# A pipeline of one pair in the expert stage: gate and up products ahead of the previous pair's down products

## The chip, the cores and the metric

The kernel runs on one core of one Trainium2 chip. The metric is the device time of one execution in microseconds (us), the median over several runs. The engines are TensorE (PE in the rows; PEld are its weight loads), VectorE (DVE), ScalarE (ACT), GpSimd (POOL) and SyncE (SP), which issues most DMA transfers.

## The reference

The reference is two whole transformer blocks on 512 tokens of width 1024 (a mixer of two recurrences with two feed-forward parts, then a state-space and a sparse-attention branch, then a mixture of experts). Only the mixture of experts at the end of the second block is touched by the change. Each token has two of 32 experts:

```python
combine = jnp.sum(jax.nn.one_hot(ids, N_EXPERTS, dtype=jnp.float32) * wts[..., None], axis=1)
out = jnp.zeros((b * s, d), jnp.float32)
for e in range(N_EXPERTS):
    he = jax.nn.silu(t @ w_g[e]) * (t @ w_u[e])
    out = out + combine[:, e:e + 1] * (he @ w_d[e])
```

The matrices w_g and w_u are 1024 x 256 and w_d is 256 x 1024, in float32, so that one expert has 3 MiB of weights and all 32 have 96 MiB. They are read once in each execution. The result is scaled by a gate row (g2 in the kernel) and added to the residual.

## The kernel before

The program is written with a planner: every instruction names its tiles, the planner works out the dependences, and it lays down the order of each engine from its own estimate of durations (`schedule_with_timeline_sim=True`), taking what stands first in the program among what it holds to be ready. An instruction can so be drawn ahead of one that stands before it in the program.

The expert stage is `Moe.experts`. Experts are worked in pairs n = 0 to 15, two pairs make a quad q, and each expert has 64 places for tokens. A pair fills the 128 partitions: places of its first expert in the lower 64, of its second in the upper 64. The steps of a pair are these:

- `gather(q)`, once for a quad: VectorE makes one-hot rows `oh` of token against place (L2089), TensorE multiplies them with token numbers and weights (the index products, L2097), and POOL fetches the rows of the tokens from `n2d` in HBM into `xr` by an indirect DMA (L2103).
- `turn(n)`: eight transposes of `xr` on TensorE (L2119), copied to `xg` (L2120).
- Gate and up products (L2143): 16 matmuls with 64-column tiles, alternating between the two experts, whose halves of the array work side by side. Each shows as two records, so a pair has 32. They fill one PSUM bank `ph`: gate in the left half, up in the right.
- `h`: silu of the gate half on ScalarE (L2147), then a product with the up half and the combine weight on VectorE (L2155).
- Four transposes of `oh` to `ohT` (L2152), and two transposes of `h` (L2158), copied to `hT` by VectorE (L2160).
- Down products (L2168): 8 matmuls with 64-column tiles (16 records) in two halves f of 512 columns. VectorE scales each by `g2` (L2171), ScalarE rounds it to `yh` (L2172), and VectorE keeps the rest as `yl` (L2173).
- After the second pair of a quad, the scatter (L2182, L2183): 32 matmuls of 128-wide tiles that add `ohT` times `yh` and `yl` of both pairs into a PSUM bank for each of eight blocks, each added to `yac` by VectorE (L2184).

PSUM has four banks with the tag pa (`ph` and the down products), three with pb (index products, half of the turns, `ohT`, `h` transposes, scatter) and one with pf (the other half of the turns).

The weights come through a ring of nine 1 MiB buffers, `ew`. Part j of the weights is pair j // 6, expert j % 2 of the pair, and within the pair two parts of gate and up (each two transfers of 512 KB, L2067) and then one of down (one transfer of 1024 KB, L2070). A tenth load takes the slot of the first when that has been used, and so on. `prefetch` asks for the first nine parts before the stage; `experts` asks for the parts of a pair at its head:

```python
for j in range(e0 * 3, e0 * 3 + 6):
    self.load(i, ew, j)
wts = [self.ewt.pop(j) for j in range(e0 * 3, e0 * 3 + 6)]
```

Between `gather(0)` and the first turn stands `then()`, a branch for experts with more than 64 tokens, whose body isn't entered here. Ahead of the stage, `tail2` stores the normed tokens to `n2d` with four transfers (L2304), from which POOL gathers.

Of the kernel before, what the change touches and what calls it, by code (L numbers as in the profile page):

```python
# [10 lines left out]
F32 = mybir.dt.float32  # L11
F32R = mybir.dt.float32r
# [3 lines left out]
AF = mybir.ActivationFunctionType  # L16
# [1943 lines left out]
class Moe:  # L1960
# [94 lines left out]
    def load(self, i, ew, j):  # L2055


        nc = self.nc
        if j >= NE * 3 or j in self.ewt:
            return  # L2060
        e, part = j // 6 * 2 + j % 2, j % 6 // 2
        t = ew.tile([128, 2048], F32, name="ew", bufs=EW)
        if part < 2:

            t = t.rearrange("p (n k m) -> p n k m", n=2, k=4)
            for n, w in enumerate(("w_exp_gate_2", "w_exp_up_2")):
                nc.sync.dma_start(t[:, n], i[w][0][e].rearrange("(p k) n -> p k n", k=8)[:, part * 4:part * 4 + 4])  # L2067
        else:
            t = t.rearrange("p (k n) -> p k n", k=2)
            nc.sync.dma_start(t, i["w_exp_down_2"][0][e].rearrange("(k p) n -> p k n", p=128))  # L2070
        self.ewt[j] = t

    def prefetch(self, i, ew):
        for j in range(EW):
            self.load(i, ew, j)

    def experts(self, i, ew, n2d, yac, xr, g2, then):

        nc, tc = self.nc, self.tc
        with tc.tile_pool(name="eb", bufs=1, reuse_waits="tile") as eb:  # L2080
            batch = []
            ohs, w2s, rows = {}, {}, {}

            def gather(q):

                oh = eb.tile([128, 4, 256], F32R, name="oh", bufs=2)
                ohs[q] = oh
                for c in range(4):
                    nc.vector.tensor_tensor(  # L2089
                        oh[:, c, :].rearrange("p (e s) -> p e s", s=CAP),  # L2090
                        self.pos[:, c, q * 4:q * 4 + 4][:, :, None].to_broadcast([128, 4, CAP]),
                        self.iota[:, None, :].to_broadcast([128, 4, CAP]), op=OP.is_equal)
                for pr in range(2):
                    n = q * 2 + pr
                    pw = self.pt("pb")
                    for c in range(4):
                        nc.tensor.matmul(pw[:, :6], oh[:, c, pr * 128:pr * 128 + 128],  # L2097
                                         self.chl[:, c, n].rearrange("p a b -> p (a b)"), start=(c == 0), stop=(c == 3))

                    ix = eb.tile([128, 16], U32, name="ix", bufs=4)[:, :1]  # L2100
                    nc.vector.tensor_scalar(ix, pw[:, 4:5], 512.0, None, op0=OP.add)
                    rows[n] = xr[:, n % 4, :]
                    nc.gpsimd.indirect_dma_start(rows[n], None, n2d, bass.IndirectOffsetOnAxis(ap=ix, axis=0),  # L2103
                                                 bounds_check=L - 1, oob_is_err=False)
                    w2 = w2s[n] = eb.tile([128, 16], F32, name="w2", bufs=4)[:, :1]
                    w4 = eb.tile([128, 16], F32, name="w4", bufs=2)[:, :4]
                    nc.vector.tensor_copy(w4, pw[:, :4])
                    for x in range(2):
                        rs = slice(x * 64, x * 64 + 64)
                        nc.vector.tensor_add(w2[rs, :], w4[rs, x:x + 1], w4[rs, 2 + x:3 + x])  # L2110

            def turn(n):

                r = rows.pop(n)
                for f in range(2):
                    p = self.pt(("pf", "pb")[f])
                    for k in range(4):
                        k4 = f * 4 + k
                        nc.tensor.transpose(p[:, k * 128:(k + 1) * 128], r[:, k4 * 128:(k4 + 1) * 128], self.ident)  # L2119
                    (nc.vector.tensor_copy if f else nc.scalar.copy)(  # L2120
                        xg4[:, n % 4, f * 4:f * 4 + 4, :], p.rearrange("p (k s) -> p k s", k=4))
            gather(0)
            then()
            self.table("silu_and_others")
            yhl = self.mo.tile([128, 2, 2, D], F32R, name="yhl", tag="H", bufs=1)
            xg4 = self.mo.tile([128, 4, 8, 128], F32, name="xg", tag="P", bufs=1)
            turn(0)
            for q in range(8):
                if q < 7:
                    gather(q + 1)  # L2130
                oh = ohs.pop(q)
                for pr in range(2):
                    e0 = q * 4 + pr * 2
                    for j in range(e0 * 3, e0 * 3 + 6):
                        self.load(i, ew, j)
                    wts = [self.ewt.pop(j) for j in range(e0 * 3, e0 * 3 + 6)]
                    ss = slice(pr * 128, pr * 128 + 128)
                    xg, w2 = xg4[:, (q * 2 + pr) % 4], w2s.pop(q * 2 + pr)

                    ph = self.pt("pa")  # L2140
                    for k in range(8):
                        for x in range(2):
                            nc.tensor.matmul(ph[x * 64:x * 64 + 64, :], xg[:, k, x * 64:x * 64 + 64],  # L2143
                                             wts[k // 4 * 2 + x][:, :, k % 4, :], start=(k == 0), stop=(k == 7),
                                             tile_position=(0, x * 64))
                    h = eb.tile([128, 256], F32, name="h", bufs=2)
                    nc.scalar.activation(h, ph[:, :256], AF.Silu)  # L2147
                    if e0 < 30:
                        turn(e0 // 2 + 1)
                    pt_ = self.pt("pb")  # L2150
                    for c in range(4):
                        nc.tensor.transpose(pt_[:, c * 128:(c + 1) * 128], oh[:, c, ss].bitcast(F32), self.ident)  # L2152
                    ohT = eb.tile([128, L], F32R, name="ohT", bufs=4)
                    nc.scalar.copy(ohT, pt_)
                    nc.vector.scalar_tensor_tensor(h, h, w2, ph[:, 256:], op0=OP.mult, op1=OP.mult)  # L2155
                    p = self.pt("pb")
                    for k in range(2):
                        nc.tensor.transpose(p[:, k * 128:(k + 1) * 128], h[:, k * 128:(k + 1) * 128], self.ident)  # L2158
                    hT = eb.tile([128, 2, 128], F32, name="hT", bufs=2)
                    nc.vector.tensor_copy(hT, p[:, :256].rearrange("p (k s) -> p k s", k=2))  # L2160
                    yh, yl = yhl[:, pr, 0, :], yhl[:, pr, 1, :]
                    for f in range(2):
                        fs = slice(f * 512, f * 512 + 512)
                        p = self.pt("pa")
                        for k in range(2):
                            for x in range(2):
                                dn = wts[4 + x]
                                nc.tensor.matmul(p[x * 64:x * 64 + 64, :], hT[:, k, x * 64:x * 64 + 64], dn[:, k, fs],  # L2168
                                                 start=(k == 0), stop=(k == 1), tile_position=(0, x * 64))
                        t = eb.tile([128, 512], F32, name="yt", bufs=2)  # L2170
                        nc.vector.tensor_mul(t, p, g2[:, fs])  # L2171
                        nc.scalar.copy(yh[:, fs], t)  # L2172
                        nc.vector.tensor_sub(yl[:, fs], t, yh[:, fs].bitcast(F32))  # L2173
                    batch.append((ohT, yh, yl))

                for c in range(4):
                    for f in range(2):
                        fs = slice(f * 512, f * 512 + 512)
                        p = self.pt("pb")
                        for n, (ohT, yh, yl) in enumerate(batch):  # L2180
                            s = slice(c * 128, (c + 1) * 128)
                            nc.tensor.matmul(p, ohT[:, s], yh[:, fs], start=(n == 0), stop=False)  # L2182
                            nc.tensor.matmul(p, ohT[:, s], yl[:, fs], start=False, stop=(n == len(batch) - 1))  # L2183
                        nc.vector.tensor_add(yac[:, c, fs], yac[:, c, fs], p)  # L2184
                batch = []

    def overflow(self, i, nT, yac, g2):

# [74 lines left out]
class Tail:  # L2263
# [21 lines left out]
    def tail2(self, i, mo, out):  # L2285
# [4 lines left out]
        yac = self.slot("yac", "B", True, F32)  # L2290
        xr = self.slot("xr", "A", True, F32)
        nc.gpsimd.memset(xr, 0.0)
        self.ewt = {}
        with tc.tile_pool(name="ea", bufs=1, reuse_waits="tile") as ea:
            self.room(mo)
            logits = self.logits(i, mo, self.nT, rt)
# [285 lines left out]
```

## Time and profile before

| what | us |
| --- | --- |
| median of 3 runs | 2822.51 |
| lowest and highest run | 2817.71 and 2826.92 |
| the profiled execution's own time | 2825.73 |
| its span | 2822.3 |
| first and last gate and up product | 2518.5 and 2793.1 |
| last scatter product starts | 2807.2 |

The span is the time from the first to the last profiled instruction; the execution's own time also holds what lies around it. TensorE is busy for 94% of the span by its records, whose ends are modelled. In the rows, a line such as L2168 is a line of the kernel before, `x16` counts records, and a text such as `[0.43 <-DVE hT L2160]` says that the engine had been idle for 0.43 us, and what ended that.

### The profile page before, as it was taken

To read this page: it belongs to the slowest core of one execution; us is meant where nothing else is said; L and a number is where in the kernel's file an instruction comes from. 1 tells how busy PE (TensorE), PEld (TensorE's weight loads), DVE (VectorE), ACT (ScalarE), POOL (GpSimd) and SP (SyncE) were. 2 spreads that over 40 slices of the span, in tenths; PEclk is the share of its full clock that TensorE was granted. 3 is DMA by queue.
4 is the path that set the end of the run, shared out by engine and by line. 5 is a ranking of instruction groups with operands and counts; after the bars stand their busy time and mean duration, and the time that the engine had idled before them with its cause. 6 is when DMAs were issued, how large, how long until landed. Compare 5 with 4: busy or idle time off the path is not lost. (4 is left out here: it accounts for less than half of the span.)

```text
span 2822.3 us, 40820 instructions
## 1 busy us (share of the span) xinstructions
PE 2664.6 (94%) x16161; PEld 2056.1 (73%) x16162; DVE 1552.3 (55%) x3022; ACT 993.5 (35%) x1786; POOL 284.6 (10%) x320
## 2 busy tenths in 40 slices
PE   7999999999998887999999899999999989979997
PEld 5788888888887765678888678777777767854443
DVE  6333333338367895554435757676667764454444
ACT  5211112225235663422223424465444443231112
POOL 2000000002001220100000101121122230010000
PEclk8999999999989998999999999999999999989999
DMA  7422222134333227832333523301234358269995
GB/s 263 150 90 68 59 61 67 46 98 119 96 100 106 65 66 259 278 97 90 100 95 90 150 83 99 91 13 36 79 101 124 97 187 255 81 244 360 363 371 196
DMA packets 340995, 380.46 MB, mean 135 GB/s; under 512 B 21817, under 2 KB 252605, under 8 KB 340546
## 3 DMA queue, kind: packets, MB, share of 16 engines
q1 hardware_dynamic: 338498, 373.63, 41.0%
q0 software_dynamic: 2304, 4.20, 0.4%
q8 instruction: 128, 2.10, 0.3%
q14 instruction: 65, 0.53, 0.1%
HBM read 352.34 MB, written 29.63 MB: 135 GB/s over the span
## 5 line engine op out<-in xcount | busy, mean ns | idle before, releaser
L193 ACT CAST whi<-wraw 128x1024 fp32r<-128x1024 f32 x277 | 285.7, 1041 | 739.6 <-PE pppa L213 327.2
L212 PE MATMUL pppa<-lath,whi 128*128 128x512 f32 (+4 forms) x1344 | 520.6, 388 | 18.8 <-ACT whi L193 5.3
L213 PE MATMUL pppa<-latl,whi 128*128 128x512 f32 (+3 forms) x1344 | 517.2, 385 | 5.9 <-DVE latl L360 3.8
L214 PE MATMUL pppa<-lath,wlo 128*128 128x512 f32 (+3 forms) x1344 | 510.6, 382 | 0.0
L194 DVE TENSOR_TENSOR wlo<-wraw,whi 128x1024 fp32r<-128x1024 f32 (+1 forms) x273 | 332.9, 1226 | 245.7 <-ACT whi L193 241.9
L212 PEld LDWEIGHTS pppa<-lath,whi 128*128 128x128 f32 (+3 forms) x1344 | 254.4, 189 | 81.4 <-ACT whi L193 11.6
L213 PEld LDWEIGHTS pppa<-latl,whi 128*128 128x128 f32 (+2 forms) x1344 | 254.1, 189 | 61.1 <-DVE latl L360 6.2
L214 PEld LDWEIGHTS pppa<-lath,wlo 128*128 128x128 f32 (+2 forms) x1344 | 253.5, 189 | 51.1 <-issue 2.7
L213 PE MATMUL pppb<-hl,whi 128*128 128x512 f32 (+1 forms) x576 | 195.7, 342 | 0.0
L212 PE MATMUL pppb<-hh,whi 128*128 128x512 f32 (+1 forms) x576 | 193.2, 345 | 0.0
L214 PE MATMUL pppb<-hh,wlo 128*128 128x512 f32 (+1 forms) x576 | 190.8, 340 | 0.0
L418 DVE SCALAR_TENSOR_TENSOR xT<-pppb,sG,xT 128x512 f32<-128x512 f32 (+1 forms) x144 | 96.7, 689 | 137.2 <-PE pppb L214 137.0
L398 DVE TENSOR_TENSOR hf<-sg,pppa 128x256 f32<-128x256 f32 (+1 forms) x68 | 39.7, 584 | 228.5 <-PE pppa L214 227.2
L212 PE MATMUL pppf<-lath,whi 128*128 128x512 f32 x320 | 128.1, 400 | 7.1 <-ACT lath L1835 3.4
L212 PE MATMUL pppa<-ctxh,whi 128*128 128x256 f32 (+1 forms) x440 | 124.8, 284 | 8.5 <-DVE W L921 8.2
L212 PEld LDWEIGHTS pppb<-hh,whi 128*128 128x128 f32 x576 | 108.3, 189 | 28.3 <-issue 5.8
L2143 PE MATMUL pppa<-ew,xg 128*64 128x512 f32 x512 | 127.3, 603 | 0.0
L214 PE MATMUL pppf<-lath,wlo 128*128 128x512 f32 x320 | 126.6, 396 | 0.6 <-DVE wlo L194 0.6
L213 PE MATMUL pppf<-latl,whi 128*128 128x512 f32 x320 | 126.7, 396 | 0.1
L213 PE MATMUL pppa<-ctxl,whi 128*128 128x256 f32 (+1 forms) x440 | 124.5, 283 | 0.3 <-POOL ctxl L358 0.3
L214 PE MATMUL pppa<-ctxh,wlo 128*128 128x256 f32 (+1 forms) x440 | 124.6, 283 | 0.0
L213 PEld LDWEIGHTS pppb<-hl,whi 128*128 128x128 f32 x576 | 108.9, 189 | 15.4 <-issue 3.4
(696 smaller groups left out, 4998.0 us busy)
## 6 DMA issues: line engine op xcount, KB each, us to landing
wraw<-in_ffn_w_dram SPq DMA_DIRECT2D x132, 512.0 KB, 4.1
wraw<-in_w_in_dram SPq DMA_DIRECT2D x102, 512.0 KB, 4.0
ew<-in_w_exp_gate_dram SPq DMA_DIRECT2D x64, 512.0 KB, 8.4
ew<-in_w_exp_up_dram SPq DMA_DIRECT2D x64, 512.0 KB, 4.7
ew<-in_w_exp_down_dram SPq DMA_DIRECT2D x32, 1024.0 KB, 11.0
mraw<-in_w_mod_dram SPq DMA_DIRECT2D x40, 512.0 KB, 6.0
wraw<-in_w_mod_dram SPq DMA_DIRECT2D x32, 512.0 KB, 4.5
mraw<-in_w_ada_dram SPq DMA_DIRECT2D x32, 512.0 KB, 5.7
```

Of the source, the lines that this page charges most:

```text
L193: nc.scalar.copy(hi[:, :n], raw[:, :n])
L194: (nc.gpsimd if pool else nc.vector).tensor_sub(lo[:, :n], raw[:, :n], hi[:, :n].bitcast(F32))
L212: nc.tensor.matmul(out, wh, xh, start=start, stop=False)
L213: nc.tensor.matmul(out, wh, xl, start=False, stop=False)
L214: nc.tensor.matmul(out, wl, xh, start=False, stop=stop)
L398: nc.vector.tensor_mul(h[:, :n], sg[:, :n], pp[1])
L418: nc.vector.scalar_tensor_tensor(x[:, o, :], p[:, :n], gate[:, o:o + 1], x[:, o, :], op0=OP.mult, op1=OP.add)
L2143: nc.tensor.matmul(ph[x * 64:x * 64 + 64, :], xg[:, k, x * 64:x * 64 + 64], wts[k // 4 * 2 + x][:, :, k % 4, :], start=(k == 0), stop=(k = ...
```

## The change

The loop over quads and pairs becomes a loop over 17 steps n. Step n runs `hidden(n)` (gate and up products, silu, turn of pair n + 1, the transposes of `oh` and `h`, the copy to `hT`) and then `output(n - 1)` (down products, scaling, rounding, and after an odd pair the scatter). `gather` stands ahead of `hidden` of an even pair, as before. The instructions themselves are the same.

The loads are asked for in the new order of use: the gate and up parts of pairs 0 and 1 (eight parts) in `prefetch`, and behind `hidden(n)` the down parts of pair n and the gate and up parts of pair n + 2. A set `ewd` keeps a part from being loaded twice. The ring still has nine buffers.

```diff
     def prefetch(self, i, ew):
-        for j in range(EW):
+        for j in range(4):
+            self.load(i, ew, j)
+        for j in list(range(6, 10)):
             self.load(i, ew, j)
...
+            def hidden(n):
+                for j in range(n * 6, n * 6 + 4):
+                    self.load(i, ew, j)
+                w = [self.ewt.pop(j) for j in range(n * 6, n * 6 + 4)]
...
+                h = eb.tile([128, 256], F32, name="h", bufs=2)
+                nc.scalar.activation(h, ph[:, :256], AF.Silu)
+                if n < 15:
+                    turn(n + 1)
...
+                hT = eb.tile([128, 2, 128], F32, name="hT", bufs=2)
+                nc.vector.tensor_copy(hT, p[:, :256].rearrange("p (k s) -> p k s", k=2))
+                hid[n] = hT, ohT
+
+            def output(n):
+                for j in range(n * 6 + 4, n * 6 + 6):
+                    self.load(i, ew, j)
+                w = [self.ewt.pop(j) for j in range(n * 6 + 4, n * 6 + 6)]
+                hT, ohT = hid.pop(n)
...
+                batch.append((ohT, yh, yl))
+                if n % 2 == 0:
+                    return
...
+                batch.clear()
+            for n in range(17):
+                if n < 16:
+                    if n % 2 == 0 and n < 14:
+                        gather(n // 2 + 1)
+                    hidden(n)
+
+                    for j in [n * 6 + 4, n * 6 + 5] + list(range(n * 6 + 12, n * 6 + 16)):
+                        self.load(i, ew, j)
+                if n:
+                    output(n - 1)
```

## Rows read from the trace of the kernel before

**Rows 1.** The page: its first line.

```profile
span 2822.3 us, 40820 instructions
```

**Rows 2.** Windows of two pairs: length, busy time (records) of each engine, clock, DMA.

```profile
core 0: us, PE busy (x) PEld busy (x) DVE busy (x) ACT busy (x) POOL busy (x), PEclk, DMA share, GB/s
...
2643.23:2680.56 37.33, 36.26 (x166) 16.46 (x164) 15.96 (x35) 5.58 (x10) 1.98 (x2) 1.00 0.93 351
2680.56:2716.35 35.79, 34.72 (x166) 16.37 (x164) 15.87 (x35) 5.58 (x10) 1.98 (x2) 1.00 0.97 366
...
sum 216.26, PE 210.75 PEld 98.00 DVE 93.31 ACT 34.08 POOL 9.90; mean PE 35.13 PEld 16.33 DVE 15.55 ACT 5.68 POOL 1.65
```

**Rows 3.** Timeline of TensorE, pairs 7 and 8: start, length, instruction, records, idle before.

```profile
2651.56 0.38 PE L2158 MATMUL pppb<-ident,h 128*128 128x128 f32 x2
2651.78 0.60 PE L2119 MATMUL pppf<-ident,xr 128*128 128x128 f32 x4
2652.14 0.48 PE L2182 MATMUL pppb<-yhl,ohT 128*128 128x512 f32 x1
...
2653.74 3.65 PE L2168 MATMUL pppa<-ew,hT 128*64 128x512 f32 x16 [0.43 <-DVE hT L2160]
2657.33 0.50 PE L2182 MATMUL pppb<-yhl,ohT 128*128 128x512 f32 x1
...
2657.99 4.50 PE L2143 MATMUL pppa<-ew,xg 128*64 128x512 f32 x18
...
2664.76 1.07 PE L2143 MATMUL pppa<-ew,xg 128*64 128x512 f32 x2
2665.76 0.51 PE L2182 MATMUL pppb<-yhl,ohT 128*128 128x512 f32 x1
...
2676.06 0.38 PE L2158 MATMUL pppb<-ident,h 128*128 128x128 f32 x2
2677.08 3.65 PE L2168 MATMUL pppa<-ew,hT 128*64 128x512 f32 x16 [0.64 <-DVE hT L2160]
2680.56 7.04 PE L2143 MATMUL pppa<-ew,xg 128*64 128x512 f32 x32
```

**Rows 4.** Waits, 2515 to 2800 us: who waited for whom, us, times, longest.

```profile
PEld pppa L2168 <- DVE hT L2160: 10.3, 13, 0.9
...
PE pppa L2168 <- DVE hT L2160: 6.0, 11, 0.6
...
PEld pppa L2143 <- DMA ew<-in_w_exp_down_dram: 2.5, 7, 0.4
...
PE pppb L2158 <- DVE h L2155: 2.0, 2, 1.0
```

**Rows 5.** Timeline of TensorE in pairs 13 and 15.

```profile
2761.05 0.48 PE L2182 MATMUL pppb<-yhl,ohT 128*128 128x512 f32 x1
...
2762.16 3.65 PE L2168 MATMUL pppa<-ew,hT 128*64 128x512 f32 x16
...
2794.73 0.44 PE L2158 MATMUL pppb<-ident,h 128*128 128x128 f32 x2 [1.00 <-DVE h L2155]
```

**Rows 6.** DMA queues, 2523.65 to 2786.69 us.

```profile
DMA packets 26320, 94.58 MB, mean 360 GB/s; under 512 B 3268, under 2 KB 3268, under 8 KB 26304
```

**Rows 7.** Windows, one of 20 us inside the stage.

```profile
2690.00:2710.00 20.00, 19.57 (x80) 8.69 (x79) 8.81 (x16) 1.96 (x4) 0.00 (x0) 1.00 1.03 409
```

**Rows 8.** The line L2067, gate and up weights: from issue to landing.

```profile
DMA to landing us min/median/max: 4.7/8.4/11.6
```

**Rows 9.** Timeline of SP's DMA issues.

```profile
2498.30 1.58 SPq L2304 DMA_DIRECT2D n2d<-n  x2
...
2657.42 0.33 SPq L2067 DMA_DIRECT2D ew<-in_w_exp_gate_dram  x1
```

**Rows 10.** Timelines of POOL and TensorE at the start of the stage.

```profile
2510.52 1.22 POOL L2103 DMA_INDIRECT xr<-n2d,ix  x1 [27.92 <-SPq L2194]
...
2515.15 1.09 PE L2119 MATMUL pppf<-ident,xr 128*128 128x128 f32 x4 [8.51 <-DMA xr<-n2d,ix]
```

More of the change, by code (lines that the diff above doesn't have):

```diff
@@ L2058, in load @@
         nc = self.nc
-        if j >= NE * 3 or j in self.ewt:
+        if j >= NE * 3 or j in self.ewt or j in self.ewd:
             return
+        self.ewd.add(j)
         e, part = j // 6 * 2 + j % 2, j % 6 // 2
@@ L2127, in experts @@
             turn(0)
[L2128 to L2141, printed above, removed]
-                        for x in range(2):
[L2143 to L2174, printed above, removed]
@@ new lines, in experts @@
+            hid, wts = {}, {}
+            def hidden(n):
+                for j in range(n * 6, n * 6 + 4):
+                    self.load(i, ew, j)
+                w = [self.ewt.pop(j) for j in range(n * 6, n * 6 + 4)]
+                xg, w2, oh = xg4[:, n % 4], w2s.pop(n), ohs[n // 2]
+                ph = self.pt("pa")
+                for k in range(8):
+                    for x in range(2):
+                        nc.tensor.matmul(ph[x * 64:x * 64 + 64, :], xg[:, k, x * 64:x * 64 + 64],
+                                         w[k // 4 * 2 + x][:, :, k % 4, :], start=(k == 0), stop=(k == 7),
+                                         tile_position=(0, x * 64))
+                h = eb.tile([128, 256], F32, name="h", bufs=2)
+                nc.scalar.activation(h, ph[:, :256], AF.Silu)
+                if n < 15:
+                    turn(n + 1)
+                pt_ = self.pt("pb")
+                for c in range(4):
+                    nc.tensor.transpose(pt_[:, c * 128:(c + 1) * 128],
+                                        oh[:, c, n % 2 * 128:n % 2 * 128 + 128].bitcast(F32), self.ident)
+                ohT = eb.tile([128, L], F32R, name="ohT", bufs=4)
+                nc.scalar.copy(ohT, pt_)
+                nc.vector.scalar_tensor_tensor(h, h, w2, ph[:, 256:], op0=OP.mult, op1=OP.mult)
+                p = self.pt("pb")
+                for k in range(2):
+                    nc.tensor.transpose(p[:, k * 128:(k + 1) * 128], h[:, k * 128:(k + 1) * 128], self.ident)
+                hT = eb.tile([128, 2, 128], F32, name="hT", bufs=2)
+                nc.vector.tensor_copy(hT, p[:, :256].rearrange("p (k s) -> p k s", k=2))
+                hid[n] = hT, ohT
@@ new lines, in output @@
+            def output(n):
[3 more added lines that the diff above has]
+                hT, ohT = hid.pop(n)
+                yh, yl = yhl[:, n % 2, 0, :], yhl[:, n % 2, 1, :]
+                for f in range(2):
+                    fs = slice(f * 512, f * 512 + 512)
+                    p = self.pt("pa")
+                    for k in range(2):
+                        for x in range(2):
+                            nc.tensor.matmul(p[x * 64:x * 64 + 64, :], hT[:, k, x * 64:x * 64 + 64], w[x][:, k, fs],
+                                             start=(k == 0), stop=(k == 1), tile_position=(0, x * 64))
+                    t = eb.tile([128, 512], F32, name="yt", bufs=2)
+                    nc.vector.tensor_mul(t, p, g2[:, fs])
+                    nc.scalar.copy(yh[:, fs], t)
+                    nc.vector.tensor_sub(yl[:, fs], t, yh[:, fs].bitcast(F32))
+                batch.append((ohT, yh, yl))
+                if n % 2 == 0:
+                    return
@@ L2179, in experts @@
                         p = self.pt("pb")
-                        for n, (ohT, yh, yl) in enumerate(batch):
+                        for m, (ohT, yh, yl) in enumerate(batch):
                             s = slice(c * 128, (c + 1) * 128)
-                            nc.tensor.matmul(p, ohT[:, s], yh[:, fs], start=(n == 0), stop=False)
-                            nc.tensor.matmul(p, ohT[:, s], yl[:, fs], start=False, stop=(n == len(batch) - 1))
+                            nc.tensor.matmul(p, ohT[:, s], yh[:, fs], start=(m == 0), stop=False)
+                            nc.tensor.matmul(p, ohT[:, s], yl[:, fs], start=False, stop=(m == len(batch) - 1))
                         nc.vector.tensor_add(yac[:, c, fs], yac[:, c, fs], p)
-                batch = []
+                batch.clear()
[8 more added lines that the diff above has]
+                    output(n - 1)
     def overflow(self, i, nT, yac, g2):
@@ L2292, in tail2 @@
         nc.gpsimd.memset(xr, 0.0)
-        self.ewt = {}
+        self.ewt, self.ewd = {}, set()
         with tc.tile_pool(name="ea", bufs=1, reuse_waits="tile") as ea:
```

## The prediction

> **What bounds the kernel now.** I read the page first: the span is 2822.3 us [rows 1], and its last ninth (2515 to 2807 us) is the expert stage, the only code that the diff touches. The windows come next, cut where the gate and up products of every second pair begin, so that one window is two pairs [rows 2]. The reader is to see a steady machine: six windows take 216.26 us, 36.04 us each, and TensorE is busy for 210.75 us of them at a granted clock of 1.00, the higher level (2.4 GHz). VectorE and ScalarE are busy for less than half of that, so neither is the bound. The DMA share is above 0.9, so the weights need a look of their own. The table of waits [rows 4] settles that TensorE does not wait for weights: the largest wait put down to a weight transfer is 2.5 us in all, of at most 0.4 us, which is the pause that stands at every change of product kind anyway. The transfers could go faster, too: a 20 us stretch moved 409 GB/s [rows 7] where the stage's mean is 360 GB/s [rows 6]. So TensorE's own stream bounds the stage, and I read it instruction by instruction [rows 3], taking the distance from one start to the next, since the ends are modelled.
>
> Three kinds of lost time are in that stream. First, the down products (L2168) wait for hT, the VectorE copy of the transposes just ahead of them. In an even pair the two h transposes start at 2676.06 and the down products at 2677.08 [rows 3]: 1.02 us, where two transposes take 0.22 us (2651.56 to 2651.78). In an odd pair a stopgap of four scatter products stands between, and still 1.60 us pass from 2652.14 to 2653.74, where the same four take 1.11 us in pair 13, which has no wait [rows 5]. Second, changes of kind. Down products followed by scatter take 3.59 us to the next start (2653.74 to 2657.33), followed by gate products 3.48 us (2677.08 to 2680.56), so going to 128-wide tiles costs 0.11 us; two scatter products take 0.46 us and 0.66 us pass before the gate products behind them (2657.33 to 2657.99), so coming back costs 0.20 us. Third, scatter products cut into the gate products of the next pair: two records at 2664.76 hold TensorE until 2665.76, 1.00 us, where two of an uncut row take 0.43 us (3.48 us over 16). The two 64-column halves, one per expert, run side by side, and the cut leaves one alone.
>
> **The change part by part.** All sums are made against the profiled execution: its span is 2822.3 us, its own time 2825.73 us, 3.2 us above the median of 2822.51 us. I take the same difference off the median.
>
> Removed: the wait for hT. In the new order the down products of pair n-1 follow the h transposes of pair n, and their hT was copied a whole set of gate products earlier. Even pairs (2, 4, ... 12): 1.02 - 0.22 = 0.80 us, less the 0.2 us that a change of kind costs anyway, is 0.6 us, six times: 3.6 us. Odd pairs with the wait (3, 5, 7, 9, 11): 1.60 - 1.11 = 0.5 us, five times: 2.5 us. Pair 14 has about half of one, 0.3 us. Together 6.4 us. The table of waits bounds it: 6.0 us on the matmul rows and 10.3 us on the weight loads [rows 4], which hold the pause of the change of kind as well, so I stay near the lower one. What is late next: nothing on VectorE waits for the moved work, and the hT copy gets some 8 us of slack.
>
> Removed too: in pairs 1 and 15 TensorE waits for h itself, 2.0 us in both [rows 4], 1.00 us in pair 15 [rows 5]. Pair 1 now has the down products of pair 0 beside it, and pair 15 those of pair 14. The h transposes can then cut into these, so I take 1.5 us of the 2.0.
>
> Added: the gather's index products (L2097) for the quads 2 to 7 stood behind the long run of scatter products, among 128-wide work. In the new order the down products of an even pair and the gate products of the next one are their neighbours, both 64 wide. That is one more change there and back, 0.11 + 0.20 = 0.3 us, six times: 1.8 us.
>
> Moved at no cost: the scatter stays behind the down products of the odd pair and ahead of the same gate products, so its cuts stay, with bounds: all of them gone saves at most about 2.3 us a window (the 1.54 us by which the fourth window is shorter than the third [rows 2], the same work with fewer cuts, and the rest in changes of kind), over seven scatters 16 us; as many again cost the same 1.5 us in each of eight, 12 us. I take 0, because both ends of each scatter have the neighbours they had.
>
> Weights: the order of fetching becomes the order of use again, and a ring of nine still hands each slot on nine loads later, so a load gets the same head start. One gate load issued at 2657.42 [rows 9] is for pair 9, whose products start at 2680.56 [rows 3], 23 us later, and the slowest such transfer landed 11.6 us after its issue [rows 8]. A window shorter by 1 us takes 1 us from a slack of about 11. SP issues the same 160 transfers; its waits are for slots, and behind it no compute engine waits. Cost 0; were the cover gone, a window would last as long as its 12.58 MB, 30.8 us at 409 GB/s, still below 35 us.
>
> Start of the stage: TensorE begins at 2515.15 when a gather by POOL, started at 2510.52 [rows 10], has landed; that waits for the token rows n2d, whose last two stores were issued at 2498.30 [rows 9], behind nine buffers of weights. The new prefetch loads eight. If the ninth falls behind the stores, 1 MB less stands ahead of them, 2.6 us at 409 GB/s. Nothing holds the ninth back, its slot being free, so I take 0 and keep 2.6 us as the gain's bound.
>
> Sum: -6.4 - 1.5 + 1.8 = -6.1 us. That makes 2819.6 us of the profiled 2825.7, and from the median 2816.4: **2816 us**. A window goes from 36.0 to about 35.2 us.
>
> A rule to weigh. The Trainium skill (DMA: Bandwidth & Descriptors, Bandwidth) says that for loads from HBM a limit of about 358 GB/s per core binds. By it the 94.58 MB of this stretch need 264 us, an estimate from that page, and the stretch has 263: nothing could be gained. The trace does not bear the rule out, with 409 GB/s for 20 us [rows 7]; by that row the same bytes need 231 us, and the sum stands.
>
> **The rivals.**
> 1. The scatter cuts fall away or grow fewer. The order on TensorE is a planner's, made from its own durations; in new company it may give the scatter an uncut run. For it: windows of the same work already differ by 1.5 us [rows 2]. Against: the cause of the cuts, waiting for the second pair's yh and yl, is unchanged. Two thirds of 16 us gone: 2816 - 10 = 2806 us.
> 2. The start comes earlier by the 2.6 us above: 2813.5 us.
> 3. Slower: the h transposes cut into the down products. Behind gate products now stand transposes, h transposes, down products of n-1. Where the planner holds h for late, it starts the down products, which are always ready, and lets h break in. Place: between the halves of one product pair. Price of one break: two halves alone, 0.85 us more (1.00 less about 0.15 for the change is a full slot for half a pair, twice), and a change there and back, 0.3 us: 1.15 us. In 16 pairs 18 us: 2816 + 18 = 2834 us. It eats the gain from 5 breaks on and makes the kernel measurably slower from 13. For it: pairs 1 and 15 show h late by 1 us where no transposes stand between [rows 5]. Against: in the odd pairs h follows twelve transposes with no pause (2651.56 [rows 3] bears no wait).
> 4. The weights bind: if the mean of 360 GB/s were a ceiling, the stretch could not shrink: 2822.5 us. The rule above says so in other words. For it: the DMA share of 0.9 and more [rows 2]. Against: rows 7 and the head start of 23 us.
> 5. The change does not do what it says: the planner already draws work ahead, and could draw pair n's down products back to where they were: 2822.5 us. Against: it takes what stands first in the program and is ready, and the down products of n-1 always are.
>
> **How the numbers follow.** Chances: the forecast 0.50 (own range 2811 to 2820, the hT term between 6.0 and 10.3 us and cuts a little either way), rival 1 0.15, rival 2 0.09, rival 3 0.14, rival 4 0.06, rival 5 0.06. About 0.3% (8.5 us) is what a measurement of this kernel can tell from no change: 2814.0 to 2831.0. Faster: 0.15 of the forecast's 0.50, all of rival 1 and most of rival 2, 0.37. Slower: most of rival 3, 0.12. Within: 0.51. The range 2805 to 2828 leaves out the far half of rival 1 and rival 3 with ten breaks and more.
>
> **What would show it.** Right: no wait of the down products for hT in the table of waits; a start of down products 0.2 to 0.3 us behind the h transposes; two-pair windows near 35.2 us; index products between down and gate products. Cuts right: as many short groups of gate products as before. Start: gather issue still near 2510.5. Wrong: groups of down products of fewer than 16 records with h transposes between them (rival 3); windows under 34 us (rival 1); waits of gate products for weights above 0.5 us (rival 4).

## The result, and the profile after

The changed kernel takes 2837.58 us (median of 8 executions, 2833.31 to 2839.84), the kernel before 2821.94 us (8 executions too, 2817.71 to 2826.92): a ratio of 1.0052 (95%: 1.0042 to 1.0062), so 15.6 us slower. The forecast was 2816 us and no measurable change. It went the way of rival 3, at 2834 us.

The page of the changed kernel begins so; span and share of TensorE answer to [rows 1] and to the table of the profile before:

```profile
span 2835.8 us, 40822 instructions
## 1 busy us (share of the span) xinstructions
PE 2678.7 (94%) x16161; PEld 2055.8 (72%) x16162; DVE 1551.1 (55%) x3022; ACT 992.8 (35%) x1786; POOL 281.9 (10%) x320
```

TensorE shows 94% as before, so the page alone hides the loss. The windows of two pairs, from the gate products of pair 2 to those of pair 14, answer to [rows 2]:

```profile
core 0: us, PE busy (x) PEld busy (x) DVE busy (x) ACT busy (x) POOL busy (x), PEclk, DMA share, GB/s
2539.81:2576.66 36.85, 36.85 (x162) 16.05 (x158) 13.60 (x29) 5.58 (x10) 1.98 (x2) 1.00 1.03 409
...
2617.15:2659.69 42.54, 42.34 (x185) 19.38 (x185) 18.41 (x48) 6.19 (x13) 3.95 (x4) 1.00 0.86 315
...
sum 229.44, PE 227.37 PEld 103.93 DVE 95.22 ACT 33.65 POOL 11.86; mean PE 37.90 PEld 17.32 DVE 15.87 ACT 5.61 POOL 1.98
```

The six take 229.44 us, 38.2 us each where 35.2 was forecast. Those of [rows 2] took 216.26, but begin one pair later; from pair 2 to pair 14 the kernel before took 218.5 us (2547.88 to 2766.40). The clock is 1.00 as before. TensorE counts as busy for all but 2 us of them: before it idled 5.5 us and was faster. The time is inside the busy records, so the timeline has to show it (down products of pair 7, gate products of pairs 8 and 9; it answers to [rows 3]; the first column is the start):

```profile
2659.69 7.09 PE L2142 MATMUL pppa<-ew,xg 128*64 128x512 f32 x32
2666.61 1.88 PE L2175 MATMUL pppa<-ew,hT 128*64 128x512 f32 x4
2668.42 0.44 PE L2158 MATMUL pppb<-ident,h 128*128 128x128 f32 x2
2668.61 0.48 PE L2190 MATMUL pppb<-yhl,ohT 128*128 128x512 f32 x1
...
2670.18 3.65 PE L2175 MATMUL pppa<-ew,hT 128*64 128x512 f32 x12
2673.76 0.74 PE L2190 MATMUL pppb<-yhl,ohT 128*128 128x512 f32 x2
2674.43 1.07 PE L2142 MATMUL pppa<-ew,xg 128*64 128x512 f32 x2
2675.43 0.73 PE L2191 MATMUL pppb<-yhl,ohT 128*128 128x512 f32 x2
...
2685.62 0.66 PE L2122 MATMUL pppb<-ident,xr 128*128 128x128 f32 x4
2686.11 0.60 PE L2151 MATMUL pppb<-ident,oh 128*128 128x128 f32 x4
2686.64 3.65 PE L2142 MATMUL pppa<-ew,xg 128*64 128x512 f32 x16
```

L2175 is the down products, L2158 the h transposes, L2142 the gate and up products, L2190 and L2191 the scatter, L2122 the turn, L2151 the transposes of `oh`. The 16 records of a pair's down products (a product leaves two) took 3.48 us to the next start before. Here four take 1.81 us (2666.61 to 2668.42) and twelve 3.58 (2670.18 to 2673.76), 5.39 us together, because the h transposes stand between. Side by side, four records would take 0.85 us and twelve 2.6. The order of the program's TensorE instructions says why. H stands for the h transposes, S6 and S2 for six and two scatter products, D6 and D7 for the down products of pairs 6 and 7, with one digit for each product, the half of the array on which it runs.

```
before   H  D6[01010101]
after    D7[00]  H  S6  D7[101101]  S2
```

Two products of the first expert run alone, one after the other; of the six that are left four belong to the second half, so two of those run alone as well. The trace bears that out: the four records from 2666.61 and the last four of the twelve start one by one, 0.43 us apart, and the eight between them in twos. Either part costs about 1.0 us. In that order the down products of 13 of the 16 pairs are cut, 11 of them with the h transposes in the cut and two (pairs 2 and 15) with other work. In the kernel before none is.

The waits between 2515 and 2815 us answer to [rows 4]: the down products' wait for hT is gone, and what is left to weights is small.

```profile
PEld pppb L2158 <- DVE h L2155: 10.5, 9, 1.8
...
PE pppb L2158 <- DVE h L2155: 2.8, 3, 0.9
...
PEld pppa L2175 <- DMA ew<-in_w_exp_up_dram: 1.1, 3, 0.4
PEld pppa L2142 <- DMA ew<-in_w_exp_gate_dram: 1.0, 4, 0.3
```

To add up the stage I take, for each stretch of records of one kind on TensorE, the distance from its start to the next start, less its records at that kind's uncut pace (0.2135 us for gate and down products, 0.2285 scatter, 0.109 transposes, 0.12 index products), from the first gate product to the last scatter product. What is left is loss: cuts, changes of kind, and waits behind that kind.

```
us lost behind         before  after
gate and up products     17.7   18.4
h transposes              5.1    0.6
scatter                  11.7   11.3
down products             1.9   21.7
other transposes          0.8    2.3
index products           -0.1   -0.2
sum                      37.1   54.1
length of the stretch   288.6  305.6
```

The stretch is 17.0 us longer. Behind down products 19.8 us are added; the other rows together fall by 2.8 us. The profiled spans differ by 13.5 us only, because in that execution of the changed kernel the stage also began 2.6 us earlier and what follows the stretch took 0.8 us less.

### The profile page after: what moved, and what is told of

The parts are those of the page before. It is cut to its first block, busy times and chain, and to the rows that moved or that the text cites. A ratio compares the mean times of both kernels' runs of the same rounds, so it can differ in the third digit from the quotient of the medians.

```text
span 2835.8 us, 40822 instructions
## 1 busy us (share of the span) xinstructions
PE 2678.7 (94%) x16161; PEld 2055.8 (72%) x16162; DVE 1551.1 (55%) x3022; ACT 992.8 (35%) x1786; POOL 281.9 (10%) x320
## 5 line engine op out<-in xcount | busy, mean ns | idle before, releaser
L2142 PE MATMUL pppa<-ew,xg 128*64 128x512 f32 x512 | 137.3, 610 | 0.0
```

## The experiments

Theory A: the changed program lets TensorE's order be cut, and a cut that leaves one half of the array alone is dear; the new pairing itself is a gain. Rival B: the new pairing or the new order of fetching itself is dear, for instance through weights. Loss and stretch below are worked out as in the table above; the medians of the kernel before that the runs had beside them were 2824.14 us for the first four and 2820.72 us for the last four.

**e1_swap: the two down parts fetched in the other order.** The half that ran ahead was that of the part fetched first.

```diff
-for j in [n * 6 + 4, n * 6 + 5] + list(range(n * 6 + 12, n * 6 + 16)):
+for j in [n * 6 + 5, n * 6 + 4] + list(range(n * 6 + 12, n * 6 + 16)):
```

> The changed kernel with one edit: of the two down parts of a pair, the part of the second expert is asked for first. Theory A (order): the planner holds the later of the two down parts for late, starts the two down products of the first expert alone, lets the h transposes break in and leaves half of TensorE idle; the cut costs about 1.9 us a pair in some ten pairs. With this edit the part that is used first is the later one, so down products start only when both are there and stay whole. A expects groups of 16 records for down products and 2820 us (2815 to 2826), since the scatter cuts stay. Theory B (weights): the weights of the new order come late on the chip itself, or collide; the edit moves no byte and changes no distance, so B expects 2834 us or more.

Measured: 2836.04 us, ratio 1.0042 (1.0031 to 1.0053). The down products are whole again in all pairs but one, their loss is 3.2 us, and yet the kernel is as slow: the loss behind gate products rose from 18.4 to 31.4 us, 6.6 of them waits for h. The trace of this kernel, in the gate products of two pairs:

```profile
2673.09 1.02 PE L2142 MATMUL pppa<-ew,xg 128*64 128x512 f32 x2
2674.05 0.73 PE L2190 MATMUL pppb<-yhl,ohT 128*128 128x512 f32 x2
...
2675.50 3.65 PE L2142 MATMUL pppa<-ew,xg 128*64 128x512 f32 x14
...
2735.69 1.07 PE L2142 MATMUL pppa<-ew,xg 128*64 128x512 f32 x2
2736.70 0.66 PE L2151 MATMUL pppb<-ident,oh 128*128 128x128 f32 x4
2737.28 7.08 PE L2142 MATMUL pppa<-ew,xg 128*64 128x512 f32 x30
2745.35 0.44 PE L2158 MATMUL pppb<-ident,h 128*128 128x128 f32 x2 [0.99 <-DVE h L2155]
```

One product alone (two records, 1.01 us), then other work, then the rest one short on the other half, and h late by 0.99 us, since the transposes that could have covered it were drawn ahead. So mending one place moved the cuts to another: my number was wrong because I took the rest of the order as given. The order of a load alone changed the order on TensorE, while in neither kernel a wait for weights exceeded 0.4 us.

**e2_pin_text: the changed kernel, TensorE held to the order in which the program is written.** Every product and transpose of the stage is kept in program order; nothing else is changed.

```diff
+            def pin(f):
+                return lambda *a, **k: tc.keep_in_program_order(f(*a, **k)) if pinned[0] else f(*a, **k)
...
-                        nc.tensor.matmul(ph[x * 64:x * 64 + 64, :], xg[:, k, x * 64:x * 64 + 64],
+                        pin(nc.tensor.matmul)(ph[x * 64:x * 64 + 64, :], xg[:, k, x * 64:x * 64 + 64],
```

> The changed kernel with TensorE's order in the stage held to the order of the program text (same-engine order only, no added wait for a result): no planner's order on this engine, so neither cut down products nor scatter cuts, but the scatter now waits for yl of the second pair. Theory A (order) expects a two-pair window of about 34.2 us (31.8 us of products, 0.9 us of changes of kind, 1.5 us of wait for yl) against 36.0 before, and 2807 us (2800 to 2815). Theory B (late or colliding weights) expects no gain over the changed kernel: 2830 us or more, with waits of gate and down products for weights.

Measured: 2805.13 us, ratio 0.9927 (0.9901 to 0.9952); two-pair windows 34.1 us. The same pairing, loads and instructions as the changed kernel, and a stretch of 272.4 us where that took 305.6. Its pairs are alike:

```profile
2667.93 7.09 PE L2088 MATMUL pppa<-ew,xg 128*64 128x512 f32 x32
2674.95 0.66 PE L2088 MATMUL pppf<-ident,xr 128*128 128x128 f32 x4
...
2676.32 0.38 PE L2088 MATMUL pppb<-ident,h 128*128 128x128 f32 x2
2676.63 3.65 PE L2088 MATMUL pppa<-ew,hT 128*64 128x512 f32 x16
2680.21 1.05 PE L2088 MATMUL pppb<-chl,oh 128*128 128x6 f32 x8
2681.20 7.09 PE L2088 MATMUL pppa<-ew,xg 128*64 128x512 f32 x32
```

32 and 16 records uncut, no idle time, down products 0.31 us behind the h transposes. Loss: 5.5 behind gate products, 2.4 behind down products, 9.7 behind scatter products, which now wait for the second pair's `yh` and `yl` (about 1.2 us a scatter), 20.9 us in all. Rival B falls with this run: pairing and order of fetching are those of the changed kernel.

**f1_cut_one and f2_cut_both: the cut put back by hand into the held order.** In f1 the h transposes stand behind two products of one half, as in the changed kernel; in f2 behind one product of each half.

```diff
+                if n:
+                    half[n - 1] = down(n - 1)
                 p = self.pt("pb")
                 for k in range(2):
...
+                for f, k, x in [(0, 0, 0), (0, 1, 0)]:
...
+                for f, k, x in [(0, 0, 1), (1, 0, 0), (0, 1, 1), (1, 0, 1), (1, 1, 0), (1, 1, 1)]:
```

This is f1: `down` issues the first list ahead of the h transposes, and the second list follows behind them; x is the expert and so the half of the array. In f2 the lists are `[(0, 0, 0), (0, 0, 1)]` and `[(0, 1, 0), (0, 1, 1), (1, 0, 0), (1, 0, 1), (1, 1, 0), (1, 1, 1)]`.

> The changed kernel held to a written order, as in the run that held it to its program's order (2805 us, two-pair windows of 34.1), with one difference: in each of 15 pairs the h transposes stand inside the down products, behind two products of the first expert's half alone, and the six left are uneven (four of the second half). Theory A (a one-sided cut leaves a half idle twice, about 1.85 us each by the rows of the changed kernel): 15 x 1.85 + 0.85 for the last pair = 28.6 us more, 2834 us, windows of 37.8. Rival (as the prediction priced a cut, 1.15 us): 15 x 1.15 = 17 us more, 2822 us. Second rival (the cut costs little and the changed kernel's time is lost elsewhere): 2806 to 2810 us.

> The same with a cut that keeps the halves paired: two products, one of each expert, then the h transposes, then six products, three of each. Theory A (only a half left alone is dear; the break itself is a change of kind there and back, 0.3 us): 15 x 0.3 = 4.5 us more than 2805, 2810 us, windows of 34.7. Rival (any break in the down products costs 1 us or more): 2820 us or more.

Measured: f1 2832.52 us, ratio 1.0033 (1.0019 to 1.0047), its stretch 27.5 us longer than that of e2 (299.9 against 272.4) for 15 cuts, 1.83 us each, with the uneven order of the last pair in it; the loss behind a single pair's down products is 2.02 us where e2 has 0.17. f2 2808.94 us, ratio 0.9961 (0.9946 to 0.9975), stretch 3.4 us longer, 0.23 us a cut. The same break in the timeline of TensorE, first in f1:

```profile
2667.82 1.93 PE L2088 MATMUL pppa<-ew,hT 128*64 128x512 f32 x4
2669.68 0.44 PE L2088 MATMUL pppb<-ident,h 128*128 128x128 f32 x2
2670.05 3.65 PE L2088 MATMUL pppa<-ew,hT 128*64 128x512 f32 x12
2673.63 0.96 PE L2088 MATMUL pppb<-yhl,ohT 128*128 128x512 f32 x3
```

The timeline of f2:

```profile
2673.84 1.08 PE L2088 MATMUL pppa<-ew,hT 128*64 128x512 f32 x4
2674.84 0.44 PE L2088 MATMUL pppb<-ident,h 128*128 128x128 f32 x2
2675.21 2.79 PE L2088 MATMUL pppa<-ew,hT 128*64 128x512 f32 x12
2677.94 1.05 PE L2088 MATMUL pppb<-chl,oh 128*128 128x6 f32 x8
```

From start to start four records take 1.86 us or 1.00, twelve 3.58 or 2.73. The break is nearly free; what costs is that the halves stop being paired. The Trainium skill (TensorEngine Tiling (Array Packing), Tiling Modes) says that a change of the tiling mode drains the engine, and gives no price; the 0.23 us a break of f2 leave room for a small one, and no run here shows a drain by itself. f1 alone brings the kernel back from a clear gain to a loss.

**f3_pin_before: the kernel before, held to its program's order in the same way** (the edit of e2 on the kernel before).

> The kernel before, held to its program's order: down products right behind their own h transposes, nothing drawn ahead. Theory A (the change itself, at a held order, is worth what the other two held kernels showed, 17 us, and the planner takes it away): 2805 + 17 = 2822 us, 1.1 us of wait for hT in every pair. Rival (the planner's order helps the kernel before by its stopgaps, so that without it the kernel is slower): 2830 us or more. Rival (the cuts cost the kernel before as much as they cost the changed one): 2810 us or less.

Measured: 2817.09 us, ratio 0.9984 (0.9975 to 0.9994), its stretch 287.3 us against 288.6 with the free order. Every pair now waits for hT:

```profile
2674.79 0.38 PE L2085 MATMUL pppb<-ident,h 128*128 128x128 f32 x2
2675.69 3.65 PE L2085 MATMUL pppa<-ew,hT 128*64 128x512 f32 x16 [0.52 <-DVE hT L2166]
...
2687.51 0.38 PE L2085 MATMUL pppb<-ident,h 128*128 128x128 f32 x2
2689.69 3.65 PE L2085 MATMUL pppa<-ew,hT 128*64 128x512 f32 x16 [1.80 <-DVE hT L2166]
```

The loss behind h transposes is 18.6 us where the free order had 5.1, and that behind gate products 5.0 where it had 17.7. So in the kernel before, the free order bought back 13.5 us of waiting for hT with 12.7 us of cut gate products and 2.5 us more behind scatter products: nearly even. The time lies between the 2822 us of theory A and the 2810 us of the last rival. In the changed kernel there is little wait to buy back (1.6 us in e2), and the cuts are almost pure loss.

**e3_pin_new and e4_pin_old: both pairings held, with the scatter moved behind the next gate products and the index products ahead of the turn.** In e4 pairing and fetching are those of the kernel before; the loop over 16 pairs below is in e4 alone, in place of the 17 steps.

```diff
                 nc.scalar.activation(h, ph[:, :256], AF.Silu)
+                if len(batch) == 2:
+                    scatter()
+                if n % 2 == 0 and n < 14:
+                    gather(n // 2 + 1)
...
+            for n in range(16):
+                for j in range(n * 6, n * 6 + 6):
+                    self.load(i, ew, j)
+                hidden(n)
+                output(n)
```

> As e2_pin_text, and the scatter is put behind the next pair's gate and up products, the index products beside the turn's transposes, so that nothing waits and a change of kind comes only where it must. Theory A expects a window of about 32.5 us and 2795 us (2790 to 2806). If transfers bind from there on (12.58 MB in a window at 409 GB/s is 30.8 us, at 360 GB/s 34.9 us), the window stops near 34 us and the time near 2806 us, with waits for weights in the table. Theory B expects 2830 us or more.

> The order of products and of loads of the kernel before (down products of a pair behind its own h transposes), with TensorE held to the text and the scatter and index products placed as in e3_pin_new: the same stream without the pipeline of one pair. If the pipeline is worth what was reckoned for it, each pair waits 0.7 us for hT here: 11 us more than e3_pin_new, about 2806 us. If the pipeline is worth nothing once the order is held (weights bind, or the wait is filled anyhow), it equals e3_pin_new within 3 us.

Measured: e3 2793.68 us, ratio 0.9895 (0.9873 to 0.9917), windows 32.6 us; it beats both kernels. e4 2810.63 us, ratio 0.9948 (0.9931 to 0.9965), windows 35.0 us. The pairing is worth 17 us here (15.0 us by the stretches), more than the 11 I expected: e4 loses 18.8 us behind its h transposes, where its down products wait for hT in every pair, up to 1.80 us, and e3 loses 1.5. Moving the scatter took its loss from 9.7 us in e2 to 2.0 in e3. e2 against f3 is the same comparison with the scatter where it was: ratios of 0.9927 and 0.9984, 16 us of 2822.

**f4_one_set: the order free, all pairs on the weights of the first pair.** 90 of the 96 loads are left out, so what it computes differs.

```diff
-        if j >= NE * 3 or j in self.ewt or j in self.ewd:
+        if j >= 6 or j in self.ewd:
...
-                w = [self.ewt.pop(j) for j in range(n * 6 + 4, n * 6 + 6)]
+                w = [self.ewt[j] for j in range(4, 6)]
...
```

> The changed kernel with its order free, but all 16 pairs use the weights of the first pair: 90 of the 96 loads are left out, so no weight can be late, neither in the planner's reckoning nor on the chip. Theory A (the planner cuts the down products because it reckons their weights late): down products whole again, their loss from 21.7 to under 5 us, gate products cut as before (loss 15 to 25 us), 2820 us. Rival W (weights are late on the chip): 2805 us or less. Rival H (the planner cuts for h, whatever the weights): still cut, 2836 us.

Measured: 2827.76 us, ratio 1.0034 (1.0023 to 1.0045), between the numbers of theory A and of rival H. No pair's down products hold h transposes any more, as theory A says, but scatter products now cut into 7 of them. Such a cut leaves one product alone on either side, and six of the seven pairs lose about 1.1 us more than an uncut one, the last 2.1 us:

```profile
2678.15 3.65 PE L2173 MATMUL pppa<-ew,hT 128*64 128x512 f32 x14
2681.73 0.51 PE L2188 MATMUL pppb<-yhl,ohT 128*128 128x512 f32 x1
...
2683.77 1.07 PE L2173 MATMUL pppa<-ew,hT 128*64 128x512 f32 x2
2684.78 0.50 PE L2188 MATMUL pppb<-yhl,ohT 128*128 128x512 f32 x1
```

Their loss is 10.0 us, not under 5, that behind gate products 17.9. The loads decide where the free order cuts, not whether. With almost no weights to fetch its stretch is still 298.0 us, 25.6 us longer than that of e2, which fetches all of them: weights on the chip are not the cause, and rival W falls.

## Why the prediction was wrong

**What bounds the kernel: right.** TensorE's own stream does. The weights do not: no wait for one exceeds 0.4 us, and leaving nearly all of them out (f4) does not bring the time of e2. The limit of some 358 GB/s that the prediction weighed (the Trainium skill, DMA: Bandwidth & Descriptors, Bandwidth) is passed again: 409 GB/s over the 36.85 us of the first window above. The same section gives that figure for two cores that stream at once, and measures more for a core alone, so it wasn't a limit for this kernel.

**The wait for hT: right, and nearly its size.** Forecast -6.4 us. The rows of [rows 4] for it have no counterpart, and the loss behind h transposes fell by 4.5 us; behind the five stopgaps of scatter products 0.5 us each is gone as well, 2.5 us. Of these 7.0 us some 1.2 are six changes of kind that now stand elsewhere, an estimate at 0.2 us each. The scatter row falls by only 0.4 us all the same, as the last scatter now waits for `yl` (0.90 and 0.71 us). At a held order the same step is worth 15 to 17 us, since there the old pairing has nothing to cover it.

**The wait for h: gone from pairs 1 and 15, back in others.** Forecast -1.5 us of 2.0. The table of waits has 2.8 us for it after, three times 0.93, in pairs 10, 12 and 14: h is late behind the first two down products now, where they ran beside the last gate products and left no cover.

```profile
2705.54 0.44 PE L2158 MATMUL pppb<-ident,h 128*128 128x128 f32 x2 [0.93 <-DVE h L2155]
```

**Index products: not tested by itself.** Forecast +1.8 us, as they would stand between two 64-wide kinds. In three of the six places they stand behind the h transposes inside the cut, 128-wide work again, and their own loss is unchanged (-0.1 and -0.2).

**The scatter cuts: right in size, not by the reason given.** Forecast 0; the loss behind gate products went from 17.7 to 18.4 us. But the neighbours didn't stay: a scatter now begins inside the cut down products (2668.61), and transposes cut into gate products too (2685.62). That the cuts can go was right as well: held, 12.9 of the 18.4 us do (e2).

**Start: right as far as it goes.** The ninth buffer's load is still issued ahead of the stores of the token rows (2491.74 and 2493.05 us), so the bound of 2.6 us was not gained that way. The first turn began 2.6 us earlier in the profiled execution, but the two stores stood 5.2 us earlier already, and over the other runs the first gate product starts anywhere from 2513 to 2520 us.

**The step that failed** is the one that moved the down products of n-1 behind the h transposes of n and took their own time as fixed, in one uncut group. The sum had no term for down products; they lost 19.8 us more. I had the mechanism as rival 3 and gave it 0.14, on the argument that in odd pairs h follows twelve transposes and is never late. That argument used the old order for the new program: the transposes were drawn into the gate products (the turn and the `oh` transposes at 2685.62 and 2686.11, ahead of 16 gate records), so nothing stood between the gate products and h but the down products. A free order keeps no cover in its place.

The size of rival 3 was off too, in two ways that nearly cancel. I reckoned 16 breaks at 1.15 us, between the halves of one pair of products. For that form the price was right: a cut that leaves one product alone on either side cost 1.1 us in f4. But there were 11 breaks with h in them, and in most of them two products of one half had run ahead, which costs 1.83 us (f1): two products alone and then two more; 2.8 us of the loss is the waiting for h. Against that, some of the price came back where the half left over ran beside gate products (last section). So it is luck that its 2834 us came as near to the measured 2837.6; its terms did not. Of the other rivals, 1 (fewer scatter cuts) and 4 (weights) did not come about, and 5 had the planner's freedom right and its direction wrong: it did not restore the old order but made a worse one.

**What stays open.** Why the free order takes two products of one half first: it follows the loads (e1, f4), though no load is late on the chip, which fits an order made from a reckoning in which they are. The reckoning itself was not read.

## What to carry to other kernels

Where products run as side-by-side halves of the array, a group of them should be entered and left with both halves level; count unpaired products, not breaks. When the order of an engine is free, a change that removes a wait can also remove what the order had been traded against: price the change at a held order first, then hold that order. And where the busy share rises with the time, as here, look at the records and the start-to-start distance instead: the engine may be busy at half width.

## What the runs showed that was not expected

The busy share can rank kernels wrongly. A window from 2520 to 2780 us (columns as in the windows above), first of the changed kernel:

```profile
2520.00:2780.00 260.00, 257.00 (x1138) 115.67 (x1135) 103.53 (x217) 38.88 (x71) 11.86 (x12) 1.00 0.92 345
```

The same window of e2:

```profile
2520.00:2780.00 260.00, 256.52 (x1238) 122.08 (x1240) 113.53 (x237) 41.60 (x75) 13.80 (x14) 0.99 0.94 366
```

Both are busy for 99% of it, but one gets through 1138 records and the other through 1238.

The two halves also pair up across kinds. Down products of one half, left over by a cut, ran beside gate products of the other half in the changed kernel:

```profile
2694.04 2.36 PE L2175 MATMUL pppa<-ew,hT 128*64 128x512 f32 x9
2695.87 0.59 PE L2142 MATMUL pppa<-ew,xg 128*64 128x512 f32 x1
2696.24 0.59 PE L2175 MATMUL pppa<-ew,hT 128*64 128x512 f32 x1
2696.30 0.59 PE L2142 MATMUL pppa<-ew,xg 128*64 128x512 f32 x1
2696.67 0.59 PE L2175 MATMUL pppa<-ew,hT 128*64 128x512 f32 x1
```

Starts come in twos, 0.06 us apart and 0.43 us from one two to the next: the pace of paired halves, 0.2135 us a record. The Trainium skill (TensorEngine Tiling (Array Packing), Tiling Modes) says that tiles work independently and in parallel, and these rows agree. So part of the cut's price came back where gate products stood next to the half left over (a loss of 0.39 us in pairs 8, 10 and 12); where scatter products did, none came back (1.97 us in pairs 5 and 7).
